# A last group of token searches moved beside the expert sums, early rows rescheduled, one more row buffer

## The chip, the cores and the metric

The kernel runs on one core of a Trainium2 chip. The metric is the device time of one launch in microseconds (us). Five engines of the core work side by side, each through its own list of instructions in order: TensorE (PE, matrix products), VectorE (DVE), ScalarE (ACT), GpSimd (POOL, which here mostly issues gathers) and SyncE (SP, which issues the other transfers). An instruction that has to wait holds up everything behind it on its own engine.

## The reference, cut to what matters

One decoder layer over 1024 tokens of width 1024: a mixing sub-layer, then a retrieval of experts. The retrieval (`peer`) is what the change touches:

```python
q = (hf @ w_query).reshape(T, PEER_HEADS, 2, D_KEY // 2)
s1 = jnp.einsum("thk,hnk->thn", q[:, :, 0], sub_keys1)
s2 = jnp.einsum("thk,hnk->thn", q[:, :, 1], sub_keys2)
v1, i1 = lax.top_k(s1, PEER_TOPK)              # 16 of 128 keys, per head and half
v2, i2 = lax.top_k(s2, PEER_TOPK)
cand = v1[..., :, None] + v2[..., None, :]     # 256 candidates
top_s, pos = lax.top_k(cand, PEER_TOPK)        # 16 experts of 16384, per head
gates = jax.nn.softmax(top_s, axis=-1)
...
u = expert_down[ib]; v = expert_up[ib]
act = jax.nn.gelu(jnp.einsum("td,thkd->thk", hb, u))
out = jnp.einsum("thk,thkd->td", gb * act, v)
```

So each token has 8 heads x 2 halves = 16 searches over 128 scores, one selection over the sums, and 128 chosen experts, each with a row of `expert_down` and one of `expert_up`.

## The kernel before, in words

The 1024 tokens are eight tiles of 128, in three groups: tiles 0 and 1, tiles 2 to 4, tiles 5 to 7. `front` handles a group at a time: the input projection and convolution, the chunked scan, two more projections (`product` with `w_z` and `w_o`), and then the **query stage**, a loop of 16 blocks that makes the scores of all tiles of the group. Each block's scores are searched at once by `top16` (five VectorE instructions), except for the tiles in `LATE`, whose scores are stored to a buffer in HBM, `scd`, and searched later by `selects`. `select` turns a tile's searches into expert numbers and gates.

The experts are summed in two ways. For the tiles in `DT` (1 to 4) every expert is computed, as dense products, in 128 **blocks** of 128 experts (`experts`); the gates are spread into a dense table `gd` beforehand, with one-hot products ("hot" builds, four VectorE instructions for eight tokens). For the tiles in `GT` (0, 5, 6, 7) only the chosen rows are fetched by indirect transfers from POOL ("gathers"). Tile 0 is done while the later groups' fronts run: `ahead` fetches its 128 pairs of half rows, first 128 products with the token (tile name `acts`, line 875), then 128 sums (line 879); these are the **early rows**. Tiles 5, 6 and 7 are gathered by `gather` beside the dense blocks: a whole row per expert, one product (line 910), a small activation, one sum (line 903). Row buffers rotate; there are `ROWBUFS`, plus `MORE` in the experts' stage.

What runs in the background is written as generators that are stepped by `drain` (a list, first come first served, at so many steps per dense block) and by `fetch` (the early rows, at `FETCH` steps per call). Each step is recorded at a lower priority, by `LATER`. The order on each engine is then decided by a list scheduler that works with priorities and its own timeline; the generators' pace does not fix it alone. In the experts' stage the number of steps per block follows from

```python
steps = 129 * len(GT) - self.taken + 40
want = min(steps * b // (NK - SB * LEAD), steps)
```

At the end, `gather` and the dense sums both call `finish`, which needs two rows (the gate and the last norm's weights) that `last_rows` loads into a row buffer.

Of the kernel before, what the change touches and what calls it, by code (L numbers as in the profile page):

```python
# [43 lines left out]
SB = 3  # L44
LEAD = 2
SOON = 2

ROWBUFS = 3
MORE = 1

# [9 lines left out]

LATE = [6, 7]

FETCH = (0, 1.6, 0.5)


class Trunk:
# [25 lines left out]
    def fetch(self, n):  # L92

        if not self.early or self.pending:
            return
        self.owed += n
        while self.owed >= 1:
            self.owed -= 1
            with self.tc.high_priority(offset=-LATER):
                if next(self.early, None) is None:  # L100
                    return
            self.taken += 1
# [604 lines left out]

    def selects(self, lp):

        for t, v, pi in self.late:  # L710
            for h in range(0, 8, 2):
                sc = lp.tile([128, 4, 128], FT, name="sc")
                self.nc.sync.dma_start(sc, self.scd[LATE.index(t), :, 2 * h:2 * h + 4])
                for b in range(4):
                    scr = self.tp.tile([128, 128], FT, name="tscr", bufs=2)
                    self.top16(sc[:, b], v[:, h + b // 2, b % 2], pi[:, h + b // 2, b % 2], scr)
                    if b % 2:
                        yield
            yield from self.select(t, v, pi)
# [14 lines left out]
    def select(self, t, v, pi):  # L734
# [5 lines left out]
        for r, rn, cn in PAIRS:  # L740
# [4 lines left out]
            else:  # L745
                for a in range(rn):
                    nc.vector.tensor_tensor(cand[:, :, o:o + cn], v[:, :, 1, :cn],
                                            v[:, :, 0, r + a:r + a + 1].to_broadcast([128, 8, cn]), op=OP.add)
                    o += cn
        key = tp.tile([128, 8, 2, 16], BF, name="key")  # L750
        nc.vector.tensor_copy(key, pi)
        yield
# [19 lines left out]
        for start, length in ROWS:  # L772
            nc.vector.tensor_scalar(q, p, float(start), float(length - (start == SINGLE)), op0=OP.is_ge, op1=OP.mult)
            nc.vector.tensor_tensor(r2, r2, q, op=OP.subtract)
            if start < SINGLE:
                nc.vector.tensor_scalar(q, p, float(start), None, op0=OP.is_ge)
                nc.vector.tensor_tensor(r1, r1, q, op=OP.add)  # L777
        yield
        idx = tp.tile([128, 2, 8, 16], FT, name="idx")
        for j, r in enumerate((r1, r2)):  # L780
            for h in (0, 4):
# [3 lines left out]
                                        r[:, hs, None, :].to_broadcast([128, 4, 16, 16]), op=OP.is_equal)  # L785
                nc.vector.tensor_tensor(oh, oh, key[:, hs, j].unsqueeze(3).to_broadcast([128, 4, 16, 16]), op=OP.mult)
                for m in (8, 4, 2):
# [100 lines left out]
    def gather(self, j):  # L888
# [28 lines left out]
        add(*prev)  # L917
        rows = self.last_rows()
        if j == len(GT) - 1:
            self.kept = rows  # L920
            self.rows.pop()
        xx = self.row()
# [25 lines left out]
    def last_rows(self):  # L948
# [3 lines left out]
        return rows  # L952

    def experts(self):

# [25 lines left out]
        self.wk = self.pool("fin", side="right")  # L981
        lp = self.pool("late", 2, reuse_waits="tile")
        self.bg += [self.early, self.mixed(self.gather(EARLY), self.selects(lp), 3)]
        self.bg += [self.gather(j) for j in range(EARLY + 1, len(GT))]
        steps = 129 * len(GT) - self.taken + 40
        gates = None
# [30 lines left out]
        for u, size in enumerate(units):  # L1017
# [28 lines left out]
            queue.append((u, ws))  # L1046
        self.drain()
        rows = self.kept
        xs = [self.residual(new(kind).bitcast(FT), t) for kind, t in zip(["raw"] * 3 + ["dnh"], reversed(DT))]
        sums = dict(held)  # L1050
        for i in reversed(range(nt)):
            mm2(*queue[0], [(i, 0), (i, 1)])
            self.finish(DT[i], [sums[i, 0], sums[i, 1]], rows, xs.pop(0), new("dnl").bitcast(FT), i < SOON)

    def run(self):
# [13 lines left out]
        self.pending = EARLY  # L1069
        self.late = []  # L1070
        self.scd = dp.tile([len(LATE), 128, 16, 128], FT, name="scd")
# [69 lines left out]
```

## Time and profile before

| | |
|---|---|
| median of 3 runs | 2901.29 us (2898.45 to 2906.26) |
| the profiled execution, whole | 2912.44 us |
| its span, first to last instruction | 2910.6 us |
| PE busy in the span | 2663.1 us (91%) |
| DVE busy in the span | 2375.6 us (82%) |
| moved by the transfers | 893.31 MB, 307 GB/s over the span |

How to read it: the span is what the rows of the trace cover; 1.8 us of the execution lie outside it. PE's busy time holds pipelined products whose ends are modelled. The stages follow each other without a barrier, so a stage's bounds are taken at a VectorE instruction that opens it: the third group's scan opens at 841 us of the span, its query stage at 1060 us, the dense blocks at 1221 us.

### The profile page before, as it was taken

What the parts mean: (1) busy time and instruction counts of PE and PEld (TensorE: products, weight loads), DVE (VectorE), ACT (ScalarE), POOL (GpSimd) and SP (SyncE); (2) the same over time, 40 slices, a digit from 0 to 9 for tenths busy, and PEclk for the clock granted to TensorE, in tenths of its full rate; (3) what the DMA queues carried; (4) which work ended last, traced back from release to release, by engine and by line L of the source; (5) the groups of instructions that cost most, each with busy time, mean ns of one, the idle gap of its engine ahead of it and who ended that gap; (6) DMA issues with size and microseconds to landing.
All of it is one profiled execution on the core that took longest, in us unless ns stands there. A gap on an engine that the chain in (4) does not pass through costs nothing. (4 is left out here: it accounts for less than half of the span.)

```text
span 2910.6 us, 31644 instructions
## 1 busy us (share of the span) xinstructions
PE 2663.1 (91%) x10243; PEld 1746.7 (60%) x10244; DVE 2375.6 (82%) x5156; ACT 830.1 (29%) x2244; POOL 884.6 (30%) x679
## 2 busy tenths in 40 slices
PE   8899986789889989699999999999999999999961
PEld 5688555676557876465655666666666666666630
DVE  6625898979999879899999777787877777778887
ACT  3523451322254342322222222222222222222211
POOL 0000066554440005022333333333333333333343
PEclk9999987899989989899999999999999999999985
DMA  8655389999863679888999999899999989998986
GB/s 304 222 172 173 103 296 331 356 362 361 289 234 124 185 220 383 277 310 323 352 354 356 356 366 337 336 364 361 346 348 351 370 320 372 348 368 339 356 320 234
DMA packets 264278, 893.31 MB, mean 307 GB/s; under 512 B 25904, under 2 KB 110000, under 8 KB 212656
## 3 DMA queue, kind: packets, MB, share of 16 engines
q0 software_dynamic: 92448, 541.11, 49.0%
q1 hardware_dynamic: 171664, 350.18, 34.7%
q8 instruction: 81, 1.33, 0.2%
q14 instruction: 85, 0.70, 0.1%
HBM read 840.86 MB, written 50.34 MB: 306 GB/s over the span
## 5 line engine op out<-in xcount | busy, mean ns | idle before, releaser
L907 POOL DMA_INDIRECT row<-in_ud,eidx x384 | 547.5, 1426 | 1105.8 <-DVE yacc L903 870.4
L903 DVE SCALAR_TENSOR_TENSOR yacc<-row,act,yacc 128x1024 f32<-128x1024 f32 x381 | 488.5, 1282 | 67.9 <-ACT act L912 65.1
L910 DVE SCALAR_TENSOR_TENSOR row<-row,h 128x1024 f32<-128x1024 f32 x384 | 467.1, 1218 | 51.1 <-DMA row<-in_ud,eidx 50.8
L1007 PE MATMUL rot<-up,w 128*128 128x512 f32 x1024 | 464.5, 596 | 4.8 <-DVE ys L1014 4.8
L1007 PE MATMUL res<-up,w 128*128 128x512 f32 x1024 | 458.6, 592 | 0.0
L870 POOL DMA_INDIRECT row<-in_ud,eidx x256 | 313.6, 1225 | 417.3 <-DVE rkb L777 102.1
L911 ACT ACTIVATE act<-act 128x1 f32<-128x1 f32 x384 | 77.1, 201 | 976.0 <-DVE row L910 975.6
L1007 PEld LDWEIGHTS rot<-up,w 128*128 128x128 f32 x1024 | 194.9, 191 | 221.8 <-issue 208.3
L1007 PEld LDWEIGHTS res<-up,w 128*128 128x128 f32 x1024 | 193.8, 189 | 200.5 <-issue 189.4
L1033 PE MATMUL m<-h2h,dnh 128*128 128x512 f32 x1024 | 292.9, 427 | 18.9 <-ACT dnh L1023 18.9
L1033 PE MATMUL m<-h2l,dnh 128*128 128x512 f32 x1024 | 285.6, 413 | 0.0
L1033 PE MATMUL m<-h2h,dnl 128*128 128x512 f32 x1024 | 279.6, 412 | 0.0
L1033 PEld LDWEIGHTS m<-h2h,dnh 128*128 128x128 f32 x1024 | 193.5, 189 | 96.8 <-issue 39.5
L307 PE MATMUL acc<-wraw,r 128*128 128x256 f32 x1024 | 239.3, 388 | 8.3 <-ACT s L525 8.3
L435 PE MATMUL acc<-r,wraw 128*128 128x384 f32 (+1 forms) x768 | 235.0, 464 | 2.3 <-ACT s L439 1.3
L581 PE MATMUL acc<-rz,wraw 128*128 128x384 f32 (+1 forms) x768 | 235.3, 457 | 0.0
L1033 PEld LDWEIGHTS m<-h2l,dnh 128*128 128x128 f32 x1024 | 192.6, 188 | 66.5 <-issue 30.4
L1033 PEld LDWEIGHTS m<-h2h,dnl 128*128 128x128 f32 x1024 | 193.4, 189 | 59.2 <-issue 19.1
L307 PEld LDWEIGHTS acc<-wraw,r 128*128 128x128 f32 x1024 | 196.3, 195 | 37.9 <-ACT s L525 9.9
L1014 DVE TENSOR_TENSOR ys<-rot,ys 128x512 f32<-128x512 f32 x168 | 115.4, 687 | 112.1 <-PE rot L1007 111.6
L435 PEld LDWEIGHTS acc<-r,wraw 128*128 128x128 f32 x768 | 147.7, 195 | 81.8 <-issue 8.6
L581 PEld LDWEIGHTS acc<-rz,wraw 128*128 128x128 f32 x768 | 143.7, 194 | 64.0 <-issue 2.3
(298 smaller groups left out, 3271.3 us busy)
## 6 DMA issues: line engine op xcount, KB each, us to landing
up<-in_ud SPq DMA_DIRECT2D x128, 512.0 KB, 7.4
raw<-in_downT SPq DMA_DIRECT2D x128, 512.0 KB, 7.9
gd<-stage SPq DMA_DIRECT2D x32, 1024.0 KB, 9.3
gates<-gd SPq DMA_DIRECT2D x16, 2048.0 KB, 12.3
wraw<-in_w_c SPq DMA_DIRECT2D x48, 512.0 KB, 5.6
wraw<-in_w_q SPq DMA_DIRECT2D x48, 512.0 KB, 6.3
wraw<-in_w_o SPq DMA_DIRECT2D x36, 512.0 KB, 5.2
row<-in_w_ada SPq DMA_DIRECT2D x32, 512.0 KB, 5.3
```

The lines of the kernel that those rows point to most:

```text
L307: self.nc.tensor.matmul(acc[i], a(4 * kp + j, slice(i * 128, (i + 1) * 128)), ws[:, j * 256:(j + 1) * 256], start=kp == kps[0] and j == 0 ...
L435: nc.tensor.matmul(acc[:, :T], wc[:, k * 128:(k + 1) * 128], h[:, k], start=k == 0, stop=k == KB - 1)
L581: nc.tensor.matmul(acc[:, :T], wq[:, k * 128:(k + 1) * 128], g[:, k], start=k == 0, stop=k == KB - 1)
L870: nc.gpsimd.indirect_dma_start(out=u[:, i * D:(i + 1) * D], out_offset=None, in_=src, in_offset=bass.IndirectOffsetOnAxis(ap=e[:, s + i:s ...
L903: nc.vector.scalar_tensor_tensor(acc, u[:, D:], a, acc, op0=OP.mult, op1=OP.add)
L907: nc.gpsimd.indirect_dma_start(out=u, out_offset=None, in_=self.I["ud"], in_offset=bass.IndirectOffsetOnAxis(ap=e[:, s:s + 1], axis=0))
L910: nc.vector.scalar_tensor_tensor(u[:, :D], u[:, :D], 1.0, h2, op0=OP.mult, op1=OP.mult, accum_out=a)
L911: nc.scalar.activation(a, a, AF.Gelu)
L1007: nc.tensor.matmul(ps, w[:, ts], up[:, hs], start=st, stop=sp, skip_group_check=True)
L1014: nc.vector.tensor_tensor(ysum[o], ps, ysum[o], op=OP.add)
L1033: nc.tensor.matmul(p1, dn[x][:, k * 128:(k + 1) * 128], h2[y][:, k], start=(k == 0 and n == 0), stop=(k == KB - 1 and n == 2))
```

## The change

`LATE` takes tile 5 as well, so that none of the last group's 48 searches is done in the query stage: all scores go to `scd`. `selects` now loads two scores at a time (a head) into a pool of one buffer, where it loaded four into a pool of two. In the experts' stage two streams of searches stand at the head of the background list: tile 5's, mixed with what is left of the early rows, and those of tiles 6 and 7, mixed with tile 5's gathers. Early rows are recorded at twice the lower priority, and `FETCH` takes fewer in the second group and more in the third. `MORE` makes five row buffers of four. `LEAD` brings the background's steps to an end 12 blocks earlier. The last dense sums are written ahead of the last `drain`. In `select`, keys are kept twice side by side so that their product runs over pairs, and one comparison and addition become one instruction.

```diff
-LEAD = 2
+LEAD = 6
-MORE = 1
+MORE = 2
-LATE = [6, 7]
-FETCH = (0, 1.6, 0.5)
+LATE = [5, 6, 7]
+FETCH = (0, 1.3, 1.1)
...
     def fetch(self, n):
-            with self.tc.high_priority(offset=-LATER):
+            with self.tc.high_priority(offset=-2 * LATER):
...
-    def selects(self, lp):
+    def selects(self, lp, late):
-        for t, v, pi in self.late:
-            for h in range(0, 8, 2):
-                sc = lp.tile([128, 4, 128], FT, name="sc")
-                self.nc.sync.dma_start(sc, self.scd[LATE.index(t), :, 2 * h:2 * h + 4])
+        for t, v, pi in late:
+            for h in range(8):
+                sc = lp.tile([128, 2, 128], FT, name="sc")
+                self.nc.sync.dma_start(sc, self.scd[LATE.index(t), :, 2 * h:2 * h + 2])
...
-        key = tp.tile([128, 8, 2, 16], BF, name="key")
-        nc.vector.tensor_copy(key, pi)
+        key = tp.tile([128, 2, 8, 16, 2], BF, name="key")
+        nc.vector.tensor_copy(key.rearrange("p j h r d -> p h j r d"), pi.unsqueeze(4).to_broadcast([128, 8, 2, 16, 2]))
...
-                nc.vector.tensor_scalar(q, p, float(start), None, op0=OP.is_ge)
-                nc.vector.tensor_tensor(r1, r1, q, op=OP.add)
+                nc.vector.scalar_tensor_tensor(r1, p, float(start), r1, op0=OP.is_ge, op1=OP.add)
...
-                nc.vector.tensor_tensor(oh, oh, key[:, hs, j].unsqueeze(3).to_broadcast([128, 4, 16, 16]), op=OP.mult)
+                pairs = oh.rearrange("p h r (a b) -> p (h r) a b", b=2)
+                nc.vector.tensor_tensor(pairs, pairs, key[:, j, hs].rearrange("p h r d -> p (h r) d").unsqueeze(2)
+                                        .to_broadcast([128, 64, 8, 2]), op=OP.mult)
...
-        rows = self.last_rows()
-        if j == len(GT) - 1:
-            self.kept = rows
-            self.rows.pop()
+        rows = self.keep() if j == len(GT) - 1 else self.last_rows()
...
+    def keep(self):
+        if self.kept is None:
+            self.kept = self.last_rows()
+            self.rows.pop()
+        return self.kept
...
-        lp = self.pool("late", 2, reuse_waits="tile")
-        self.bg += [self.early, self.mixed(self.gather(EARLY), self.selects(lp), 3)]
+        lp = self.pool("late", reuse_waits="tile")
+        self.bg += [self.mixed(self.early, self.selects(lp, self.late[:1]), 2),
+                    self.mixed(self.gather(EARLY), self.selects(lp, self.late[1:]), 3)]
...
-        self.drain()
-        rows = self.kept
+        rows = self.keep()
...
             self.finish(DT[i], [sums[i, 0], sums[i, 1]], rows, xs.pop(0), new("dnl").bitcast(FT), i < SOON)
+        self.drain()
```

What the scheduler made of it is seen in the order of instructions, at three places. In the names, `hot` are the one-hot builds, `yacc<-row,acts` an early sum, `v<-sc` the first step of a search, `raw<-in_downT` the load of a dense block's weights, `sc<-scd` the load of stored scores.

The first place is VectorE at the end of the third group's query stage. Before, early sums, builds and tile 5's searches alternate:

```order
L879 SCALAR_TENSOR_TENSOR yacc<-row_9912,acts,yacc 128x1024
L826 TENSOR_TENSOR hota<-keyno,etr 128x1024
L827 TENSOR_TENSOR hotb<-keyno,etr 128x1024
L879 SCALAR_TENSOR_TENSOR yacc<-row_9912,acts,yacc 128x1024
L828 TENSOR_TENSOR hotc<-hotb,etr 128x1024
L829 TENSOR_TENSOR hotb<-hotb,etr 128x1024
L879 SCALAR_TENSOR_TENSOR yacc<-row_9955,acts,yacc 128x1024 x2
L826 TENSOR_TENSOR hota<-keyno,etr 128x1024
L827 TENSOR_TENSOR hotb<-keyno,etr 128x1024
L932 TENSOR_TENSOR row_9963<-yacc,row_9960 128x512 x2
L702 MAX v<-sc 128x8
```

Now the stage is nearly all builds; the last five early sums and the first search stand behind the last build:

```order
L829 TENSOR_TENSOR hotc<-hotb,etr 128x1024
L830 TENSOR_TENSOR hotb<-hotb,etr 128x1024
L880 SCALAR_TENSOR_TENSOR yacc<-row_9391,acts,yacc 128x1024
L880 SCALAR_TENSOR_TENSOR yacc<-row_9410,acts,yacc 128x1024 x2
L880 SCALAR_TENSOR_TENSOR yacc<-row_9415,acts,yacc 128x1024 x2
L930 TENSOR_TENSOR row_9473<-yacc,row_9470 128x512 x2
L702 MAX v<-sc 128x8 x2
L703 MATCH_REPLACE tscr<-v,sc 128x128
```

Of the 128 early sums 38 stood in this stage, and 6 stand in it now; 35 more stand in the third group's scan and projections (44, of 9 before).

The second place is SyncE's queue where the dense blocks begin. Before, the first weights stand behind the stores of tile 0's result:

```order
L1029 DMA up<-in_ud 128x1024 x6
L848 DMA gd<-stage 128x16x128
L942 DMA out<-row_9963 128x512 x2
L1021 DMA raw<-in_downT 128x1024
L1027 DMA gates<-gd 128x4096
L1021 DMA raw<-in_downT 128x1024 x2
L1027 DMA gates<-gd 128x4096
L713 DMA sc<-scd 128x512 x2
L1021 DMA raw<-in_downT 128x1024 x4
```

Now they stand behind two loads of scores, and loads of scores alternate with them from there on:

```order
L1035 DMA up<-in_ud 128x1024 x5
L849 DMA gd<-stage 128x16x128
L713 DMA sc<-scd 128x256
L849 DMA gd<-stage 128x16x128
L713 DMA sc<-scd 128x256
L1027 DMA raw<-in_downT 128x1024
L1033 DMA gates<-gd 128x4096
L1027 DMA raw<-in_downT 128x1024 x2
L713 DMA sc<-scd 128x256
L1033 DMA gates<-gd 128x4096
L940 DMA out<-row_9473 128x512 x2
```

Eight loads of four scores have become 24 loads of two, and each but the first waits for the VectorE instruction that ends the search of the one ahead of it, since there is one buffer.

The third place is VectorE at the end, where the last gathers meet the last dense sums (`dnl<-rot,row` is the first step of `finish` for a dense tile). Before:

```order
L910 SCALAR_TENSOR_TENSOR row_18526,act<-row_18526,h_16017 128x1024
L932 TENSOR_TENSOR dnl<-rot,row_18534 128x512 x2
L903 SCALAR_TENSOR_TENSOR yacc<-row_18526,act,yacc 128x1024
L932 TENSOR_TENSOR row_18537<-yacc,row_18534 128x512 x2
L936 TENSOR_REDUCE sums<-sums 128x1 x2
```

Now:

```order
L911 SCALAR_TENSOR_TENSOR row_17954,act<-row_17954,h_15587 128x1024
L904 SCALAR_TENSOR_TENSOR yacc<-row_17947,act,yacc 128x1024
L930 TENSOR_TENSOR dnl<-rot,row_17962 128x512 x2
L904 SCALAR_TENSOR_TENSOR yacc<-row_17954,act,yacc 128x1024
L930 TENSOR_TENSOR row_17965<-yacc,row_17962 128x512 x2
L934 TENSOR_REDUCE sums<-sums 128x1 x2
```

The order of these is as it was. What differs is how many gathers are left there: behind the last dense gating (`w<-w,gates`) 29 sums of gathers stood before, and 41 stand now.

## Rows read from the trace of the kernel before

**Rows 1.** The page, part 1: busy us of each engine, its share of the span.

```profile
PE 2663.1 (91%) x10243; PEld 1746.7 (60%) x10244; DVE 2375.6 (82%) x5156; ACT 830.1 (29%) x2244; POOL 884.6 (30%) x679
```

**Rows 2.** Busy time by stage: stretch, its us, engines, PE clock, DMA share, GB/s.

```profile
357.00:637.00 280.00, 219.74 (x1078) 166.81 (x1076) 252.75 (x495) 94.57 (x287) 164.65 (x135) 0.85 0.94 335
637.00:841.00 204.00, 188.75 (x667) 115.65 (x668) 197.70 (x661) 59.43 (x124) 95.13 (x83) 0.95 0.89 316
841.00:1060.00 219.00, 200.87 (x1166) 158.91 (x1167) 186.04 (x550) 91.48 (x285) 13.34 (x13) 0.90 0.55 168
1060.00:1221.00 161.00, 129.49 (x771) 91.45 (x770) 140.65 (x384) 54.39 (x107) 45.51 (x38) 0.89 0.89 300
1221.00:1310.00 89.00, 88.65 (x290) 56.79 (x291) 84.47 (x269) 20.63 (x43) 14.98 (x15) 0.96 0.86 326
1310.00:1513.00 203.00, 199.60 (x639) 120.53 (x638) 195.94 (x509) 50.60 (x130) 69.36 (x47) 0.99 0.91 340
1513.00:2810.00 1297.00, 1295.62 (x4186) 788.61 (x4184) 1024.77 (x1316) 304.17 (x820) 439.48 (x309) 1.00 0.92 352
2810.00:2907.00 97.00, 9.97 (x18) 3.87 (x16) 76.42 (x138) 18.51 (x66) 39.25 (x28) 0.56 0.70 265
...
575.00:637.00 62.00, 52.09 (x301) 45.34 (x298) 49.55 (x105) 13.96 (x39) 31.50 (x27) 0.97 1.04 387
```

**Rows 3.** PE's waits from 1060 to 1222 us: total, times, longest.

```profile
PE m L1033 <- ACT dnh L1023: 18.9, 1, 18.9
PE g L843 <- DVE tok L365: 4.8, 1, 4.8
```

**Rows 4.** SyncE's queue, in order of time: start, length, transfer.

```profile
1210.81 4.10 SPq L942 DMA_DIRECT2D out<-row  x2
1214.96 0.45 SPq L1021 DMA_DIRECT2D raw<-in_downT  x1
```

**Rows 5.** VectorE's groups by line: count, busy us, mean ns, idle before.

```profile
L879 DVE SCALAR_TENSOR_TENSOR yacc<-row,acts,yacc 128x1024 f32<-128x1024 f32 x127 | 161.2, 1269 | 4.6 <-DMA row<-in_ud,eidx 4.0
...
L826 DVE TENSOR_TENSOR hota<-keyno,etr 128x1024 f16<-128x1024 f16 x64 | 43.6, 685 | 22.6 <-PE g L843 20.7 <-ACT etr L808 1.7
...
L786 DVE TENSOR_TENSOR oh<-oh,key 128x1024 bf16<-128x1024 bf16 x32 | 39.0, 1219 | 0.3
L706 DVE FIND_INDEX8 pi<-v,tscr 128x8 uint32<-128x128 f32 x128 | 35.3, 280 | 0.0
L705 DVE FIND_INDEX8 pi<-v,sc 128x8 uint32<-128x128 f32 x128 | 35.1, 281 | 0.0
L703 DVE MATCH_REPLACE8 tscr<-v,sc 128x128 f32<-128x128 f32 x128 | 34.6, 271 | 0.0
L704 DVE MAX8 v<-tscr 128x8 f32<-128x128 f32 x128 | 33.1, 277 | 0.0
...
L702 DVE MAX8 v<-sc 128x8 f32<-128x128 f32 x128 | 29.8, 277 | 25.2 <-ACT sc L602 25.1
...
L776 DVE TENSOR_SCALAR rkd<-rka 128x128 bf16<-128x128 bf16 x56 | 10.9, 195 | 0.8
```

**Rows 6.** The loads of stored scores (line 713): durations, first and last start; landing.

```profile
L713 SPq DMA_DIRECT2D sc<-scd x8: 327/327/496, 1219.9 to 1353.8; - x8
...
DMA to landing us min/median/max: 3.1/7.6/15.7
```

**Rows 7.** Dense splits by tile, then gathered sums from 2793 us on: ns min/median/max, starts.

```profile
L1024 DVE TENSOR_TENSOR dnl<-raw,dnh x128: 1197/1221/2317, 1221.5 to 2777.5; 128x1024 fp32r<-128x1024 f32 x128
...
L903 DVE SCALAR_TENSOR_TENSOR yacc<-row,act,yacc x29: 1276/1284/1967, 2792.9 to 2882.0; 128x1024 f32<-128x1024 f32 x29
```

**Rows 8.** VectorE in order of time behind the last dense block: start, us, instruction, [idle].

```profile
2811.38 1.23 DVE L910 SCALAR_TENSOR_TENSOR row<-row,h 128x1024 f32<-128x1024 f32 x1 [1.37 <-DMA row<-in_ud,eidx]
...
2819.97 1.29 DVE L903 SCALAR_TENSOR_TENSOR yacc<-row,act,yacc 128x1024 f32<-128x1024 f32 x1 [0.60 <-ACT act L912]
...
2824.50 1.22 DVE L910 SCALAR_TENSOR_TENSOR row<-row,h 128x1024 f32<-128x1024 f32 x1 [2.10 <-DMA row<-in_ud,eidx]
```

More of the change, by code (lines that the diff above doesn't have):

```diff
@@ L706, in top16 @@
         nc.vector.max_index(pos[:, 8:], out[:, 8:], scr)
-    def selects(self, lp):
-        for t, v, pi in self.late:
-            for h in range(0, 8, 2):
-                sc = lp.tile([128, 4, 128], FT, name="sc")
-                self.nc.sync.dma_start(sc, self.scd[LATE.index(t), :, 2 * h:2 * h + 4])
-                for b in range(4):
+    def selects(self, lp, late):
[3 more added lines that the diff above has]
+                self.nc.sync.dma_start(sc, self.scd[LATE.index(t), :, 2 * h:2 * h + 2])
+                for b in range(2):
                     scr = self.tp.tile([128, 128], FT, name="tscr", bufs=2)
-                    self.top16(sc[:, b], v[:, h + b // 2, b % 2], pi[:, h + b // 2, b % 2], scr)
-                    if b % 2:
-                        yield
+                    self.top16(sc[:, b], v[:, h, b], pi[:, h, b], scr)
+                yield
             yield from self.select(t, v, pi)
@@ L981, in experts @@
         self.wk = self.pool("fin", side="right")
-        lp = self.pool("late", 2, reuse_waits="tile")
-        self.bg += [self.early, self.mixed(self.gather(EARLY), self.selects(lp), 3)]
+        lp = self.pool("late", reuse_waits="tile")
+        self.bg += [self.mixed(self.early, self.selects(lp, self.late[:1]), 2),
+                    self.mixed(self.gather(EARLY), self.selects(lp, self.late[1:]), 3)]
         self.bg += [self.gather(j) for j in range(EARLY + 1, len(GT))]
-        steps = 129 * len(GT) - self.taken + 40
+        steps = 129 * len(GT) - self.taken + 16 * len(LATE)
         gates = None
@@ L1069, in run @@
         self.pending = EARLY
-        self.late = []
+        self.late, self.kept = [], None
         self.scd = dp.tile([len(LATE), 128, 16, 128], FT, name="scd")
```

## The prediction, made before the changed kernel ran

> **What bounds the kernel now.** I read the page first, then busy time by stage, then PE's waits where the dense blocks begin, and last VectorE in order of time at the end. The page names PE, at 91% of the span, with VectorE next [rows 1]; the stages say where that average hides something [rows 2]. From 1513 to 2810 us PE is busy for 1295.6 of 1297 us at a granted clock of 1.00 (its 2.4 GHz level): the dense blocks go at PE's pace, (2777.5 - 1221.5) / 127 = 12.25 us each from the first split to the last [rows 7], and VectorE's share of 1025 us there has room. Nothing the change does to VectorE's work in that stretch can shorten it. Two other parts decide. Ahead of the blocks, from 357 to 1221 us, PE and VectorE are both near full: VectorE has 253 of 280, 198 of 204, 186 of 219 and 141 of 161 us, and PE is idle for 60, 15, 18 and 32 us [rows 2]. Behind them, from 2810 us, PE has 10 us of work in 97 [rows 2]: what runs there is gathers left over, and then the last sums. So the end is the start of the blocks, plus PE's 1589 us (1221 to 2810), plus what is left over.
>
> **The change part by part.** I count instructions in the order of the two programs and price them from rows.
>
> 357 to 637 us (second group's scan and projections): 121 early products stand here instead of 128, and 27 fewer small steps of selection. A product costs about what an early sum does, 1.27 us [rows 5], so 7 x 1.2 + 27 x 0.3 = 16 us less for VectorE. It is nearly the bound, but the transfers run at 335 GB/s in the stretch and at 387 GB/s in its last 62 us, the highest of any stage here [rows 2], and the bytes stay nearly the same. Bounds -16 (VectorE alone) and 0 (transfers alone); I take -6.
>
> 637 to 841 us: three more products, three fewer sums, 15 more small steps. VectorE is full, so 0 to +3; I take +1.
>
> 841 to 1060 us (third group's scan and projections): 44 early sums instead of 9, that is 35 x 1.27 = +44 us [rows 5]; 8 fewer build instructions (x 0.69 = -5.5) and 36 fewer steps of selection (some -12). Net +27. VectorE's idle time is 219 - 186 = 33 us, PE's 18 [rows 2]. If it all falls into idle time it costs 0, if none does +27; I take +8, nearer the lower end because the total still fits.
>
> 1060 to 1221 us (third query stage): 32 fewer early sums (-41 us), 12 of 16 searches gone, each five instructions of 277, 271, 277, 281 and 280 ns [rows 5], 1.39 us (-17), the steps of a whole selection gone (-18), 8 more build instructions (+5.5). Sum -70 us by durations, -63 counted from start to start, since neighbours overlap a little. VectorE falls from 141 to some 75 us of 161, and PE is the limit. PE has 129.5 us of work there; of the 32 us it idles, 18.9 are one wait at the end, for the first dense weights [rows 3]. These were issued at 1214.96 us, behind the stores of tile 0's result at 1210.81 us [rows 4]. In the new order they stand behind a load of scores that waits for the first search, which stands behind the last build, five early sums (6.3 us), the two first steps of the finish (1.4) and two searches run into each other (2.8). With a landing of 3.1 to 7.6 us [rows 6] and the split by ScalarE that is 15 to 19 us behind the last build: the wait of 18.9 us stays, with another reason. So -13 for the other idle time and -1 for this one, -14; bounds -32 (no idle time left) and 0.
>
> Start of the blocks: -6 + 1 + 8 - 14 = **-11 us**, bounds -48 and +30.
>
> The single buffer of scores: of the 24 loads the first 16 fall into the first eight blocks or so. Each waits for the end of the search ahead, and VectorE's order has on average 2.8 us of other work between that end and the first use of the next load. A round trip took 3.1 to 15.7 us before, median 7.6, at twice the size [rows 6], and there VectorE never waited for one, since two buffers covered it. So VectorE would stand idle for 16 x (3.1 - 2.8) = 5 us up to 16 x (7.6 - 2.8) = 77 us. Queued behind each waiting search are the split of the weights (line 1024) and the gating of the blocks, for which PE waits. The cover: the work of these eight blocks is 8.5 us less than before, and VectorE had 4.5 us idle of 89 [rows 2], so 13 us go free. I take a round trip of 4.2 us, near the low end, because no gathers run yet in these blocks and a load is half as large: 16 x 1.4 - 13 = **+9 us**; bounds 0 and +64. From 1310 to 1513 us VectorE was full before (196 of 203 [rows 2]); its work there is the same by count, with more search and fewer gathers. That is where the debt arises: by every later block some 13 gathers fewer are done than before.
>
> The end: behind the last dense gating 41 sums of gathers stand instead of 29. The 29 took from 2792.9 us to the end of the last, which started at 2882.0 and took up to 1.97 us, 91 us in all [rows 7]. Four gathers take 13.1 us (2811.38 to 2824.50), of which 2.1 are a wait for a gathered row, once in four, and 0.6 a wait for the activation [rows 8]. With four buffers the wait for the row comes round once per buffer; the fifth should take some of it. Bounds: 13.1 / 4 = 3.28 us a gather if it helps nothing, (13.1 - 2.1) / 4 = 2.76 us if the row is never late. I take 2.85: 41 x 2.85 = 117, against 91: **+26 us**, bounds +22 and +43. The Trainium skill ("DMA: Bandwidth & Descriptors", section "Where 436 GB/s comes from") gives about 358 GB/s as a core's limit from HBM; by it a gather of 1.05 MB cannot go below an estimated 2.93 us, and the term would be +29. The trace has 387 GB/s over 62 us [rows 2], above that figure, so I keep the rows' bound.
>
> No price: the pairs make a product of 1.22 us cost about 0.69, as the builds with the same layout do [rows 5], and 56 instructions of 0.2 us fall away; where this lies ahead of the blocks it is in the sums above, beside the blocks PE covers it [rows 2] (if PE were not the limit there, 12 products would be worth 6 us). `LEAD` and the moved `drain` change nothing I can find: the first step of the last dense sums still stands between the last two gathers. The five-buffer gathers are not the pace beside the blocks, where PE is.
>
> Sum: -11 + 9 + 26 = **+24 us**. The profiled execution took 2912.4 us, so 2936; the median of the runs shown is 11 us lower, which gives **2925 us**. This likeliest case alone spans 2900 to 2950.
>
> **The rivals.** (a) *VectorE alone sets the start* (the other side). From 357 us on it has 16 - 3 - 27 + 63 = 49 us less to do ahead of the first split. If PE's idle time follows all of it, the start moves by -49 and the score loads stay hidden: -49 + 26 = -23, 2878 us. It decides from a start 35 us earlier on (-35 + 26 = -9). For it: VectorE's share of 88 to 97% in three of the four stretches. Against it: most of it, the 63, comes from the query stage, where PE has 129.5 of 161 us and the rest is mostly the wait for the weights. (b) *The score loads are the new wait*: at the median landing they cost +64, so -11 + 64 + 26 = +79, 2980 us. It decides at about 6 us a round trip. For it: the landings [rows 6] and a queue in which weights that wait for their buffer stand ahead of scores. Against it: no gathers in those blocks, and 3.1 us seen. The Trainium skill ("Trainium Kernel Development and Optimization", section "Best Practices") asks for double buffers so that transfers and computing overlap; by that rule the loss of the second buffer shows as such a bubble. No row before has a single buffer, so the trace only bounds it. (c) *The gathers left over are just paid for*: all of the query stage's idle time goes, -32 - 6 + 1 + 8 = -29, the loads are hidden, and the end costs +26: -3, within 0.3%, 2898 us.
>
> **How the numbers follow.** Likeliest case 0.45, (a) 0.22, (b) 0.15, (c) 0.18. About 0.3% (9 us) is what a measurement of this kernel tells from no change. Slower: the likeliest case, less a sliver that ends within 0.3%, and (b), 0.58. Faster: (a) and a little of (c), 0.23. Same: 0.19. The range takes in (c), the likeliest case, the inner edge of (a) and the lower half of (b): 2880 to 2965.
>
> **What would show it.** The first split at 1205 to 1215 us. VectorE some 40% idle in the query stage, with PE still waiting 15 to 20 us ahead of the first dense product. VectorE waiting for `sc<-scd` in the first eight blocks, 5 to 40 us in all. Blocks at 12.25 us as before. 41 gathered sums behind the last gating, at 2.75 to 3.0 us each. I am wrong if the first split comes before 1186 us, if VectorE waits over 60 us for scores, or if the gathers left over take under 95 us.

## The result and the profile after

The changed kernel takes 2950.32 us (median of 4 runs, 2949.27 to 2952.09) against 2901.87 us for the kernel before (4 runs, one more than in the table above): 1.0167 times as long, 95% interval 1.0149 to 1.0184, or 48 us more. The prediction was 2925 us: the direction was right, the loss half of what it is. One execution each of two variants below, of 11748.53 and 6954.96 us beside nine ordinary ones, stands in no ratio given here.

The profiled execution has a span of 2947.9 us. Line numbers of the code around the change have moved (the early sum is now line 880, the split 1030, the gathered sum 904); a split is VectorE's first step on a dense block's weights. The page's first part:

```profile
PE 2655.7 (90%) x10244; PEld 1738.6 (59%) x10244; DVE 2349.2 (80%) x5100; ACT 830.1 (28%) x2245; POOL 904.1 (31%) x679
```

PE's busy time is 7 us less than before [rows 1] and VectorE's 26 us less, so the time went into waits. The first and the last split, then the gathered sums behind the last gating, answer to [rows 7] (a tile's view, then a line's, of the changed kernel):

```profile
L1030 DVE TENSOR_TENSOR dnl<-raw,dnh x128: 1195/1219/1228, 1234.1 to 2786.4; 128x1024 fp32r<-128x1024 f32 x128
```

```profile
L904 DVE SCALAR_TENSOR_TENSOR yacc<-row,act,yacc x41: 1274/1284/1965, 2804.6 to 2919.2; 128x1024 f32<-128x1024 f32 x41
```

So the blocks began at 1234.1 us instead of 1221.5 (+12.6), took 1552.3 us from first to last split instead of 1556.0 (-3.7), and from the last split to the end it took 161.5 us instead of 133.1 (+28.4). That makes +37 against the profile shown before. That profile was itself a long one: its execution took 2912.44 us, 11 more than the median. A second one of the same kernel (2898.85 us, 3 under the median) has a span of 2897.1 us and these splits:

```profile
L1024 DVE TENSOR_TENSOR dnl<-raw,dnh x128: 1199/1222/2316, 1211.2 to 2766.7; 128x1024 fp32r<-128x1024 f32 x128
```

Against it the three parts are +22.9, -3.2 and +31.1, together the 51 us between the two spans.

Busy time by stretch of the changed kernel, cut at the bounds that its trace shows: the third group's projections, the step to the query products, these products, the step to the first dense product; then the first blocks, the blocks up to 1513 us, the rest of them, and the end. Columns as in [rows 2].

```profile
905.00:1058.00 153.00, 136.84 (x826) 118.00 (x825) 131.47 (x303) 48.44 (x119) 32.24 (x24) 0.91 0.74 235
1058.00:1077.00 19.00, 11.20 (x105) 9.82 (x103) 16.77 (x43) 9.69 (x20) 0.58 (x1) 0.64 0.91 292
1077.00:1192.00 115.00, 113.85 (x662) 77.97 (x661) 46.58 (x73) 39.48 (x79) 1.19 (x1) 1.00 0.62 186
1192.00:1235.00 43.00, 10.26 (x105) 8.71 (x104) 28.32 (x71) 10.18 (x19) 6.64 (x10) 0.59 1.00 321
...
1234.00:1313.00 79.00, 78.00 (x267) 51.31 (x268) 65.26 (x335) 17.94 (x23) 0.00 (x0) 0.98 0.46 165
1313.00:1513.00 200.00, 197.13 (x624) 117.91 (x623) 197.29 (x576) 48.22 (x122) 69.04 (x47) 0.99 0.92 349
1513.00:2820.00 1307.00, 1306.42 (x4223) 795.80 (x4221) 1031.91 (x1332) 306.18 (x828) 448.63 (x312) 1.00 0.91 352
2820.00:2944.00 124.00, 9.52 (x16) 3.88 (x16) 106.02 (x174) 24.40 (x90) 57.98 (x39) 0.55 0.79 303
```

The same stretches of the kernel before, at its own bounds:

```profile
907.00:1047.00 140.00, 133.20 (x853) 116.02 (x852) 116.71 (x323) 48.37 (x117) 0.00 (x0) 0.98 0.55 159
1047.00:1066.00 19.00, 10.46 (x104) 9.47 (x103) 17.05 (x45) 9.79 (x23) 0.55 (x1) 0.66 0.88 283
1066.00:1181.00 115.00, 112.06 (x602) 75.36 (x601) 100.25 (x185) 35.71 (x70) 45.23 (x34) 0.97 0.90 318
1181.00:1222.00 41.00, 13.23 (x135) 11.87 (x134) 37.25 (x190) 13.64 (x26) 0.28 (x4) 0.73 0.86 265
...
1221.00:1300.00 79.00, 78.65 (x267) 52.42 (x268) 74.47 (x229) 19.78 (x41) 13.12 (x13) 0.96 0.85 321
```

Three things are to be seen. The projections, where early sums now stand, became 13 us longer, and PE idles 16 of 153 us there instead of 7 of 140. The query products took 115 us both times, with VectorE busy for 100 us of them or for 47: PE is full in both. It made 60 more products there in the changed kernel, about what the projections (27) and the step behind (30) had lost, but none of the four stretches got shorter by it. And in the first 79 us of the blocks the transfers moved 165 GB/s instead of 321, with no work on POOL: the gathers need the results of tile 5's searches, and the first one is issued at 1329.1 us, 95 us after the first split; in the kernel before it was 26 us after. PE's waits of the changed kernel, in the projections and from there to the first dense product:

```profile
PE g L844 <- DVE hotb L830: 7.9, 5, 3.2
PE g L844 <- DVE hotc L829: 4.8, 3, 1.8
PE acc L307 <- ACT s L525: 2.7, 1, 2.7
...
PE m L1039 <- ACT dnh L1029: 20.8, 1, 20.8
```

In the projections PE waits for one-hot builds (lines 829 and 830), which stand among early sums on VectorE, and for no transfer. Before, these two waits were shorter:

```profile
PE g L843 <- DVE hotb L829: 2.8, 2, 1.7
PE g L843 <- DVE hotc L828: 1.0, 1, 1.0
```

The wait for the first dense weights stayed (20.8 us, 18.9 before [rows 3]). SyncE's queue of the changed kernel, in order of time, shows its new reason: the weights stand behind the second load of scores, which waits for the first search.

```profile
1210.98 6.50 SPq L713 DMA_DIRECT2D sc<-scd  x1
1217.53 0.43 SPq L849 DMA_DIRECT2D gd<-stage  x1
1222.65 0.32 SPq L713 DMA_DIRECT2D sc<-scd  x1
1224.23 0.33 SPq L1027 DMA_DIRECT2D raw<-in_downT  x1
```

### The profile page after: what moved, and what is told of

The parts are those of the page before. It is cut to its first block, busy times and chain, and to the rows that moved or that the text cites. A ratio compares the mean times of both kernels' runs of the same rounds, so it can differ in the third digit from the quotient of the medians.

```text
span 2947.9 us, 31644 instructions
## 1 busy us (share of the span) xinstructions
PE 2655.7 (90%) x10244; PEld 1738.6 (59%) x10244; DVE 2349.2 (80%) x5100; ACT 830.1 (28%) x2245; POOL 904.1 (31%) x679
## 4 chain that ended last, share of the span: by engine, by line
PE 66%; DVE 15%; DMA 7%; issue 5%; POOL 4%; ACT 2%; SPq 0%; POOLq 0%; DVEq 0%; ACTq 0%
PE m L1039 22%; PE rot L1013 14%; PE res L1013 13%; PE acc L307 7%; PE acc L581 5%; DMA row<-in_ud,eidx 2%; DVE yacc L880 2%; PE acc L435 2%; POOL row L908 2%; POOL row L871 2%; DVE row L876 1%; PE g L844 1%; DMA gd<-stage 1%; DVE s L470 1%; DVE tscr L703 1%
## 5 line engine op out<-in xcount | busy, mean ns | idle before, releaser
L908 POOL DMA_INDIRECT row<-in_ud,eidx x384 | 561.4, 1462 | 1104.3 <-DVE yacc L904 914.9
L871 POOL DMA_INDIRECT row<-in_ud,eidx x256 | 321.0, 1254 | 525.4 <-ACT sc L602 106.8
L1039 PE MATMUL m<-h2h,dnh 128*128 128x512 f32 x1024 | 292.5, 427 | 20.8 <-ACT dnh L1029 20.8
```

Source lines behind the costliest of these rows:

```text
L871: nc.gpsimd.indirect_dma_start(out=u[:, i * D:(i + 1) * D], out_offset=None, in_=src, in_offset=bass.IndirectOffsetOnAxis(ap=e[:, s + i:s ...
L908: nc.gpsimd.indirect_dma_start(out=u, out_offset=None, in_=self.I["ud"], in_offset=bass.IndirectOffsetOnAxis(ap=e[:, s:s + 1], axis=0))
L1039: nc.tensor.matmul(p1, dn[x][:, k * 128:(k + 1) * 128], h2[y][:, k], start=(k == 0 and n == 0), stop=(k == KB - 1 and n == 2))
```

## The experiments

Times of runs of the kernel before that were made beside the experiments: 2901.49 us (19 runs) beside the two variants of the early rows' schedule, the one of tile 5's searches and the paired keys alone; 2897.71 us (13 runs) beside the two with four row buffers, the last dense sums ahead and the second profile; 2896.76 us (9 runs) beside the other three. Ratios are to these.

**A second profile of the kernel before** (no edit).

> The kernel before, profiled a second time, because its first profiled execution was 11 us longer than the median of its runs. Expected: a span of 2893 to 2905 us; if the third group's projections (907 to 1047 us in the first profile) are where executions differ, they take 128 to 135 us here instead of 140, and the rest agrees within 2 us.

The span is 2897.1 us, so the first profile was a long one. The projections are not where: they took 139 us again (900 to 1039 us). Of the 13.5 us between the two, 7 had arisen ahead of the projections, 10.3 by the first split, and 2.7 came behind the last one.

**Only the early rows rescheduled.** The kernel before with

```diff
-FETCH = (0, 1.6, 0.5)
+FETCH = (0, 1.3, 1.1)
-            with self.tc.high_priority(offset=-LATER):
+            with self.tc.high_priority(offset=-2 * LATER):
```

> The kernel before with only the early rows rescheduled as in the change (twice the lower priority, fewer in the second group, more in the third). Theory A: the dense blocks began 12.6 us late because early sums moved into the third group's projections push the one-hot builds, and with them TensorE's products, into the query stage, where TensorE is the limit. Then the first split comes at 1229 to 1238 us, 29 sums stand behind the last gating as before, and the time is 9 to 15 us above before (2911 to 2917). Theory B: the start is late because of the moved searches and their loads of scores ahead of the first dense weights. Then the first split stays at 1218 to 1225 us and the time within 5 us of before.

2921.27 us, 1.0069 times before (1.0045 to 1.0093). First split at 1228.5 us, 17.3 later than in the second profile of before and half a microsecond under A's range; 29 sums behind the last gating. Theory A holds and B falls, though the loss of 20 us is above the range given. Busy time by stretch (query products, then the step to the first dense product), and PE's waits from 905 to 1230 us:

```profile
1056.00:1169.00 113.00, 111.84 (x630) 75.95 (x629) 74.34 (x197) 38.06 (x76) 5.58 (x4) 1.00 0.61 183
1169.00:1229.00 60.00, 28.82 (x250) 23.40 (x249) 56.72 (x204) 20.47 (x39) 0.28 (x4) 0.60 0.77 233
```

```profile
PE g L843 <- DVE hotc L828: 14.1, 5, 5.4
PE g L843 <- DVE hotb L829: 11.4, 9, 2.2
```

The place differs from the changed kernel's: here the builds that the early sums displaced come out behind the query products, in a step of 60 us instead of 41. The price is the same kind: PE waits for builds, 25.5 us in all, where it was 13.8 us before.

**Early rows scheduled as before, the rest as changed.**

```diff
-FETCH = (0, 1.3, 1.1)
+FETCH = (0, 1.6, 0.5)
-            with self.tc.high_priority(offset=-2 * LATER):
+            with self.tc.high_priority(offset=-LATER):
```

> The changed kernel with the early rows scheduled as before. In its order 49 sums stand behind the last gating and 26 early sums behind the first split. Theory A: the start comes back to 1205 to 1222 us although all 48 searches stand behind it; from the last split to the end 175 to 185 us (49 sums at 2.75); time 2935 to 2955. Theory B: the start stays at 1230 to 1238 us, time 2955 to 2975.

2957.43 us (1.0193, 1.0174 to 1.0213), 2 us above the range of A; first split 1215.3 us and 181.7 us from the last split to the end, both as A has them. The start comes back although all 48 searches still stand beside the blocks. But 26 early sums stand there now too, and against the changed kernel the 19 us won at the start are lost again: 5 us in the blocks and 20 us at the end. The run is 7 us slower. The projections and the query products of this run, and its PE waits, first in the projections and then up to the first dense product:

```profile
902.00:1029.00 127.00, 126.75 (x830) 111.59 (x829) 96.94 (x245) 44.25 (x114) 0.00 (x0) 1.00 0.57 167
1049.00:1165.00 116.00, 115.73 (x677) 79.37 (x676) 48.78 (x75) 40.65 (x81) 1.42 (x1) 0.99 0.63 187
```

```profile
PE acc L307 <- ACT s L525: 0.2, 1, 0.2
...
PE m L1039 <- ACT dnh L1029: 36.1, 1, 36.1
```

Without early sums the projections take 127 us, PE waits 0.2 us in them, and the granted clock is 1.00. In the changed kernel they take 153 us: 16 us of PE's idle time, and 10 us more busy time for about the same number of products (136.8 for 826, 126.8 for 830) at a granted clock of 0.91. The wait for the first weights has grown to 36 us. SyncE's queue shows what stands ahead of them, a load of scores whose issue alone took 17.8 us:

```profile
1184.03 17.82 SPq L713 DMA_DIRECT2D sc<-scd  x1
1206.53 0.33 SPq L1027 DMA_DIRECT2D raw<-in_downT  x1
```

Whether weights issued ahead of the scores would by themselves start the blocks sooner was not tried.

**Tile 5's searches back in the query stage.** The changed kernel with

```diff
-LATE = [5, 6, 7]
+LATE = [6, 7]
-        self.bg += [self.mixed(self.early, self.selects(lp, self.late[:1]), 2),
-                    self.mixed(self.gather(EARLY), self.selects(lp, self.late[1:]), 3)]
+        self.bg += [self.early, self.mixed(self.gather(EARLY), self.selects(lp, self.late), 3)]
-        steps = 129 * len(GT) - self.taken + 16 * len(LATE)
+        steps = 129 * len(GT) - self.taken + 40
```

> The changed kernel with tile 5's searches back in the query stage (LATE holds tiles 6 and 7 alone), all else as changed. Its order has 26 sums behind the last gating. Theory of the tail (the gathers are paced by transfers beside the blocks, so what is not gathered in the first eight blocks is left over): the 161 us from the last split to the end become 115 to 125. Theory A on the start: it stays late, first split at 1228 to 1238 us, time 2885 to 2900. Theory B: the start comes back to 1215 to 1222 us, time 2875 to 2885. If the tail were longer for another reason (the order of the last dense sums, five buffers), it would stay above 140 us and the time above 2915.

2906.72 us (1.0018, 1.0006 to 1.0031): 44 us less than the changed kernel. The first split stays late (1235.1 us) and the end shrinks from 161.5 to 118.7 us. So the searches make the end and the early rows make the start. The time is 7 us above the range, but the parts given beside it do not add up to that range: a start at 1228 to 1238 us, the blocks' 1552 us and an end of 115 to 125 us are 2895 to 2915 us.

**The early sums kept in the query stage, the rest as changed**, with the early rows' schedule of before, and

```diff
-    def row(self):
+    def row(self, own=False):
         self.rows.append(self.rows.pop(0))
+        while own and self.rows[-1] >= ROWBUFS + MORE - 1:
+            self.rows.append(self.rows.pop(0))
...
-        return (self.gp if i < ROWBUFS else self.more).tile(
+        return (self.gp if i < ROWBUFS else self.more if i == ROWBUFS else self.more2).tile(
...
-                    u = self.row()
+                    u = self.row(True)
...
+        self.more2 = self.pool("more2", reuse_waits="tile")
```

> The changed kernel with the early rows scheduled as before and kept in the third query stage (they use the first four row buffers only, and the fifth lies in a pool of its own): 38 early sums in the query stage as before, all 48 searches of the last group beside the blocks, 41 sums behind the last gating. It shows what moving tile 5's searches alone is worth. Theory: TensorE sets the length of the query stage, so 12 searches less there win nothing, and the gathers that start later are paid for at the end: first split 1208 to 1218 us, 158 to 164 us from the last split to the end, time 2920 to 2932 us. Rival: VectorE sets the query stage once the early sums are there again; then the first split comes before 1203 us and the time is 2903 to 2914 us.

2928.28 us (1.0107, 1.0092 to 1.0123), 22 us less than the changed kernel. The first split comes at 1209.8 us, 1.4 us from the second profile of before: twelve searches less in the query stage win nothing there. The end takes 161.2 us, as in the changed kernel.

**Four row buffers instead of five**, the rest as changed.

```diff
-MORE = 2
+MORE = 1
```

> The changed kernel with four row buffers instead of five, all else as changed. Its order has 43 sums behind the last gating, against 41. Theory: a gather behind the blocks takes 2.86 us with five buffers and 3.15 with four, because the wait for a gathered row comes round once per buffer; 43 sums then take 135 us instead of 115, and the time is 2965 to 2972 us. Rival: the pace is set by the transfers whatever the buffers; then 2.86 us each, 2954 to 2958 us.

2970.59 us, 20 us more than the changed kernel. The 43 sums of this run (its line 904, behind the last gating):

```profile
L904 DVE SCALAR_TENSOR_TENSOR yacc<-row,act,yacc x43: 1280/1283/1970, 2810.2 to 2941.9; 128x1024 f32<-128x1024 f32 x43
```

That is (2941.9 - 2810.2) / 42 = 3.14 us each, against (2919.2 - 2804.6) / 40 = 2.87 with five: the theory holds for the pace. VectorE waits 14.8 us for gathered rows among these sums, 3.8 us among the 41 of the changed kernel. Only 12.6 of the 20 us are at the end, though: the blocks took 15.4 us longer and began 6.8 us sooner, so it is luck that the time fell into the range.

**Four row buffers and two score buffers**, the rest as changed.

```diff
-MORE = 2
+MORE = 1
-        lp = self.pool("late", reuse_waits="tile")
+        lp = self.pool("late", 2, reuse_waits="tile")
```

> The changed kernel with four row buffers and two buffers for the stored scores, to be set against the run with four row buffers and one score buffer. If the single buffer costs time in the first blocks, VectorE's waits for stored scores (14.5 us in the changed kernel) fall below 5 us and the first 16 blocks end 5 to 12 us sooner than with one. If the waits are covered, the blocks take the same time within 2 us, and the time differs only by the three more sums that its order leaves behind the last gating (46 against 43), 8 to 10 us longer.

2964.43 us. VectorE's waits for scores are 0.5 us here, 10.1 us with one score buffer and four row buffers (8.2 of them in the first sixteen blocks), and 14.5 us in the changed kernel (4.9 behind the first split). A tile's view of this run, then of the changed kernel:

```profile
  DMA sc<-scd: 0.5, 2
```

```profile
  DMA sc<-scd: 14.5, 10
```

The seventeenth split comes 180.4 us after the first, 191.7 us with one score buffer, and the last split 1554.0 us after the first, 1567.7 us with one: beside four row buffers the second score buffer is worth 11 to 14 us of the blocks, of which 10 go again into the three more sums at the end. But the changed kernel, with one score buffer and five row buffers, needs 181.2 us to the seventeenth split, and the kernel before needed 180.6: there the waits cost nothing.

**Only the paired keys and the fused comparison**, on the kernel before: of the change's diff the lines in `select` alone, of which the product is

```diff
-                nc.vector.tensor_tensor(oh, oh, key[:, hs, j].unsqueeze(3).to_broadcast([128, 4, 16, 16]), op=OP.mult)
+                pairs = oh.rearrange("p h r (a b) -> p (h r) a b", b=2)
+                nc.vector.tensor_tensor(pairs, pairs, key[:, j, hs].rearrange("p h r d -> p (h r) d").unsqueeze(2)
+                                        .to_broadcast([128, 64, 8, 2]), op=OP.mult)
```

> The kernel before with only the paired keys and the fused comparison. 32 products of 1.22 us become about 0.69, and 56 instructions of 0.2 us go, 28 us of VectorE's work in all, some 10 of it beside the dense blocks and 7 in the third query stage. If VectorE's work ahead of the blocks sets their start: 10 us faster. If it does not (TensorE or transfers do): within 5 us of before. The order has 29 sums behind the last gating, as before.

2896.16 us, 0.9981 times before (0.9967 to 0.9995). The product fell from 1219 to 684 ns as expected. The projections became 11 to 12 us shorter by it (128 us, from 905 to 1033 us, at a granted clock of 1.00), but the query products behind them took 120 us, with PE waiting 6.9 us for transfers of keys, and the first split came at 1215.2 us, between those of the two profiles of before. So VectorE's work alone does not set the start.

**Paired keys, and the last dense sums really ahead of the gathers.** In the kernel before, with the paired keys, the change's loads of two scores into one buffer and its moved `drain`, the two rows of the last finish go to buffers of the dense weights instead of a gather's row buffer:

```diff
     def keep(self):
         if self.kept is None:
-            self.kept = self.last_rows()
-            self.rows.pop()
+            self.kept = self.new("up"), self.new("up")
+            self.bcast(self.kept[0], self.rowd[5])
+            self.bcast(self.kept[1], self.I["norm_final"])
         return self.kept
...
         add(*prev)
+        while j == len(GT) - 1 and self.kept is None:
+            yield
```

> The kernel before with the paired keys and fused comparison, and with the two rows of the last finish in two buffers of the dense blocks' weights instead of a gather's row buffer, so that in the order the dense tiles' finish stands between the gathers that are left over; 29 sums behind the last gating as before. Theory C: the finish came last because its rows waited for a buffer that the last gathers use. Then TensorE's wait of 70 to 100 us for the first step of the finish is gone, the 27 us from the last gathered sum to the end fall to 10 to 15, the finish steps lengthen the gathers by some 5 to 12 us, and the time is 2884 to 2893 us (against 2896 with the paired keys alone). Rival: VectorE is the limit behind the blocks, so the finish only changes places and the time stays at 2893 to 2898 us.

2897.51 us (0.9988, 0.9973 to 1.0004): the rival holds. PE's wait of 69 us (with the paired keys alone) for the first step of the finish is gone, and from the start of the last gathered sum to the end it takes 15 us instead of 29. But the 29 sums lie between 2781.5 and 2882.4 us, 3.60 us each instead of 3.13 with the paired keys alone. So it was the row buffer that held the finish back, which is why writing it ahead of the last `drain` moved nothing; and moving it is worth nothing: VectorE does that work either way, which fits the unchanged time.

**Paired keys and the fifth row buffer alone**: the kernel before with the paired keys, the loads of two scores that make room, and the early sums kept in the query stage by `row(own)` and `more2` as above.

```diff
-MORE = 1
+MORE = 2
...
-        lp = self.pool("late", 2, reuse_waits="tile")
+        lp = self.pool("late", reuse_waits="tile")
+        self.more2 = self.pool("more2", reuse_waits="tile")
```

> The kernel before with the paired keys, the fused comparison and the fifth row buffer (with the loads of two scores in one buffer that make room for it), tile 5's searches and the early sums left in the query stage; 26 sums behind the last gating. Theory: the start stays at 1211 to 1218 us, the blocks at 1552 to 1556 us, and from the last split to the end it takes 116 to 121 us instead of 130 to 133, so the time is 2883 to 2891 us, faster than both. If the fifth buffer is worth nothing without the rest, 2895 to 2900 us.

2880.49 us, 0.9946 times before (0.9932 to 0.9959), 2.5 us under the range: the lowest median of all, 70 us less than the changed kernel. First split at 1211.6 us, 1547.6 us of blocks (4 us less than expected), 119.0 us at the end. This kernel too has a single score buffer, for 16 loads.

**The same with the last dense sums ahead of the gathers**, by the edit of `keep` and the `while` above, and `LEAD` as in the change:

```diff
-LEAD = 2
+LEAD = 6
```

> The run before this one, and with the dense tiles' finish between the last gathers (its rows in two buffers of the blocks' weights), and the steps spread as in the change; 27 sums behind the last gating. With four buffers the 12 us of finish steps between the gathers gave back all that was won behind the last sum. If VectorE and the activations between product and sum set the pace there, it is the same with five: within 4 us of the run before this one. If the waits for gathered rows left room with four buffers and less is left with five, it is 3 to 8 us longer.

2882.27 us, within 2 us of the run before: with five buffers too, the place of the finish is worth nothing.

**The two main parts side by side.** Four of the kernels above have the paired keys, the loads of two scores into one buffer and five row buffers, and differ in where tile 5's searches and the early rows stand (us):

| | early rows as before | early rows rescheduled |
|---|---|---|
| tile 5's searches in the query stage | 2880.49 | 2906.72 |
| tile 5's searches beside the blocks | 2928.28 | 2950.32 |

Rescheduling the early rows costs 26 or 22 us and moving the searches 48 or 44 us, each about the same with and without the other. As ratios to the runs of before made beside each it is 21 or 17 us, and 47 or 43 us. (The first of the four lacks `LEAD` and the moved `drain`; the run with them and with the finish's rows moved, 2882.27 us, is within 2 us of it.) Their splits, in the order of the table's rows:

```profile
L1027 DVE TENSOR_TENSOR dnl<-raw,dnh x128: 1203/1222/1243, 1211.6 to 2759.1; 128x1024 fp32r<-128x1024 f32 x128
L1029 DVE TENSOR_TENSOR dnl<-raw,dnh x128: 1195/1222/1227, 1235.1 to 2787.0; 128x1024 fp32r<-128x1024 f32 x128
L1033 DVE TENSOR_TENSOR dnl<-raw,dnh x128: 1206/1224/1270, 1209.8 to 2766.0; 128x1024 fp32r<-128x1024 f32 x128
L1030 DVE TENSOR_TENSOR dnl<-raw,dnh x128: 1195/1219/1228, 1234.1 to 2786.4; 128x1024 fp32r<-128x1024 f32 x128
```

## Why the prediction was wrong

**The start of the blocks: -11 forecast, +12.6 measured, and +22.9 against the second profile. This is the step that failed.** Up to the projections, at 905 us, nothing can be told: -5 stood there, and the two profiles of before reach them at 907 and at 900 us. Two terms behind it did not hold.

In the third query stage I took -14, -13 of them for "the other idle time", after noting myself that PE would be the limit. The idle time was read from an average over 161 us [rows 2]. Cut at 1066 and 1181 us it lies elsewhere: PE idles 3 us of the 115 us of query products, 9 of the 19 us ahead of them and 28 of the 41 behind them. In those 41 us it waited 18.9 us for the first weights, 4.7 for builds and 4.1 for transfers of keys. In the changed kernel, with the early sums and searches out of VectorE's way, it waits 20.8 us for the first weights (that this wait stays was forecast), 5.5 for builds and 6.4 for ScalarE's copies of their products: none of it got shorter. From the end of the projections to the first split it took 174 us before and 176 after. The run that kept the early sums in the query stage and moved only the searches shows the same from the other side.

In the third group's projections I took +8, "nearer the lower end because the total still fits", and 13 us came. Here too an average misled: of VectorE's 33 idle us only 23 lay in the 140 us in which PE needs its builds. The 26 early sums that went there (33 us of work) delayed builds that PE multiplies, PE idled in short waits, and its granted clock fell from 0.98 to 0.91. The 13 us are a net figure: three runs with the paired keys and no early sums there take 128 us for the projections, so the sums cost 25 us and the keys gave 12 back. In the whole time, moving early sums out of the query stage costs 20 us in the kernel before, and moving them back wins 22 us in the changed one.

**The single score buffer: +9 forecast, none measured.** VectorE did wait, 14.5 us in ten waits, but 9.6 us of it in two waits ahead of the first split, while PE waited for the first weights. In the blocks eight waits took 4.9 us in all, just under the 5 to 40 us that I named, where the term had 16 of 1.4 us. My cover was too small as well: I counted 13 us, but with no gathers in the first eight blocks VectorE had only 65 us of work in 79. The ninth split comes 77.4 us after the first in both kernels. The rule of the Trainium skill that asks for double buffers ("Trainium Kernel Development and Optimization", section "Best Practices"), on which rival (b) rested, agrees with the run with four row buffers, where a second score buffer won 11 us by the seventeenth split, and not with the changed kernel, where the 4.9 us lay under other slack.

**The end: +26 forecast, +28.4 measured.** 41 sums at 2.87 us, where 2.85 stood; VectorE in order of time shows why the fifth buffer helps:

```profile
2814.15 2.68 DVE L904 SCALAR_TENSOR_TENSOR yacc<-row,act,yacc 128x1024 f32<-128x1024 f32 x2
2816.75 1.22 DVE L911 SCALAR_TENSOR_TENSOR row<-row,h 128x1024 f32<-128x1024 f32 x1
...
2818.57 1.28 DVE L904 SCALAR_TENSOR_TENSOR yacc<-row,act,yacc 128x1024 f32<-128x1024 f32 x1 [0.60 <-ACT act L913]
...
2821.60 1.28 DVE L904 SCALAR_TENSOR_TENSOR yacc<-row,act,yacc 128x1024 f32<-128x1024 f32 x1 [0.60 <-ACT act L913]
...
2825.09 2.68 DVE L904 SCALAR_TENSOR_TENSOR yacc<-row,act,yacc 128x1024 f32<-128x1024 f32 x2
```

Four gathers take 10.94 us, and the wait for a gathered row [rows 8] is mostly gone: 3.8 us in all among the 41 sums, 10.8 us among the 29 before. The estimate of 2.93 us from the figure of 358 GB/s in the Trainium skill ("DMA: Bandwidth & Descriptors", section "Where 436 GB/s comes from") lies above what was measured: 128 rows of 2048 numbers are 1.05 MB, and in 2.87 us that is 366 GB/s.

The term has two parts of opposite sign, which I did not price apart. Undoing the moved searches alone took 44 us off, most of it at the end (42.8); the fifth buffer by itself gave some back there (12.6). The debt itself is read from the first blocks: (321 - 165) GB/s x 79 us = 12.3 MB, twelve gathers that were not made there. It is never worked off: ahead of the 33rd split 70 gathers are issued instead of 82, from there to the last split 273 in both kernels, and behind it 41 instead of 29; the transfers run at 352 GB/s from 1513 us on in both kernels. Whether the transfers or the order set that pace was not tried.

**The rivals.** (a) needed a start 35 us earlier on, (b) cost at the first blocks, (c) a start 29 us earlier on: none of the three came. (The 88 to 97% that (a) names as VectorE's share is 87 to 97% by [rows 2].) The case that came, in which at the start the rescheduled early rows cost more than the moved searches free, had no place among them.

**What was luck.** Of the three terms only the end came about as forecast, and it carries the direction; the start went the other way. Against the second profile the errors partly cancel, 34 us too little for the start and 5 for the end, 12 us too much for the blocks.

## What to carry to other kernels

Cut a stage where the limiting engine changes its work before crediting idle time to an edit: an average over a stage spreads the idle time of its edges over a middle that has none. Work recorded at low priority still holds up the instructions behind it in an in-order queue (here 26 sums of 1.27 us, and 25 us of the projections), so filler belongs where the limiting engine takes nothing from that queue. And when two streams share the transfers, look at what the slower one fails to move while it waits for its first indices: at a fixed pace afterwards, that debt stands at the end, gather for gather (here twelve fewer early, twelve more at the end).

## What was not expected of the hardware

PE's short waits seem to cost twice: in the projections 11 waits of 16.2 us in all, none over 3.2 us, went with a granted clock of 0.91 and 10 us more of PE's busy time, beside a stretch of the same work with 0.2 us of waits and a granted clock of 1.00. The 0.91 is an average of the clock's two levels. Cut into slices of 10 us, the stretch shows a clock of 0.50, the 1.2 GHz level, for 20 us on end, after PE's busy time had fallen; it comes back while PE is busy again (columns as in [rows 2]; one earlier slice, from 915 us, has 0.83):

```profile
955.00:965.00 10.00, 6.86 (x56) 5.76 (x55) 9.85 (x23) 3.73 (x11) 6.16 (x4) 0.97 0.99 312
965.00:975.00 10.00, 4.49 (x34) 3.24 (x34) 10.00 (x22) 2.28 (x4) 0.75 (x1) 0.50 0.94 310
975.00:985.00 10.00, 5.50 (x47) 4.55 (x47) 10.00 (x25) 3.72 (x6) 0.00 (x0) 0.50 0.74 215
985.00:995.00 10.00, 10.00 (x66) 9.06 (x65) 10.00 (x29) 5.43 (x10) 0.00 (x0) 0.84 0.37 105
```

No run changed the waits without moving other work, so that the waits bring the low clock is what these stretches suggest, not what they prove.
